# Spreading the dense work of a decoder evenly beside its expert gathers, and tying VectorE's part of each dense step behind the dot of the gather ahead of it

## The chip, the cores and the metric

The kernel runs on one core of one Trainium2 chip. The metric is the device time of one execution in microseconds (us). A run of this kernel can tell a change of about 0.2% from none.

## The reference

Two layers, 512 tokens of width 1024, float32. Each layer is a token mixer and a retrieval of experts, both closed by a LayerNorm:

```
m  = x @ w_in                                   # 7168 columns: q, k, v, two LRU branches, two gates
ya = DiffAttention(q, k, v)                     # 8 heads, two softmax maps each
yr = RG-LRU(conv4(x-branch)) * gelu(gate branch)
x  = LayerNorm(alpha*x + (sigmoid(ga)*(ya@w_br_attn) + sigmoid(gr)*(yr@w_br_lru)) @ w_out)
# PEER: 8 heads; top 16 of 128 first keys, top 16 of 128 second keys, top 16 of their sums
e, g = chosen experts (16 per head, 128 per token), softmax of their scores
x  = LayerNorm(alpha*x + sum_e g[e] * gelu(x . peer_u[e]) * peer_v[e])
```

Each token thus reads 128 rows of `peer_u` and `peer_v`. The two tables lie side by side in one table `uv` of 2048 columns.

## The kernel before

Tokens stand in four blocks of 128. One gather is one indirect DMA (L819): for one of the 128 expert places it brings a row of `uv` to each of the 128 tokens of a block, 128 x 2048 floats. There are 2 layers x 4 blocks x 128 = 1024 gathers, in eight buffers (`gather`, tag `uv`). VectorE forms the dot with x (L822); for each pair of gathers ScalarE takes the gelu (L829), VectorE multiplies by g (L784), and the second half of the row is added up with that weight, either on VectorE (`acc`, L790) or on ScalarE and TensorE together (a diagonal matrix `dg`, L794, and two matmuls into `pv`, L796). `Load` keeps rough sums of TensorE's, VectorE's and the DMA's work and decides which of the two (L788). A pair is finished after the first dot of the next pair has been written.

The dense work is everything else: the mixer of a pair of blocks (projections L253 and L275, attention L349 on, LRU L459 on, gated merge L524 on), and the route (L673): queries (L656), key scores (L663), the sixteen best of each (`top16`, L710 on) and the choice of the sixteen best sums (`choose`, L723 on: candidate sums L736, three operations of 128 x 864 per head at L753, L756 and L758, and the cast L761 that writes the indices `e` which the gathers read). The route scores both blocks of a pair and chooses for the first of them; `route_late` chooses for the second.

Three generators are interleaved in `run` (L841 on): the gathers, `dense()`, and `late()`. Each dense step yields when it would like to come, in gathers. `PLAN` gives the bounds for each pair of blocks: mixer from j0 to j1, route to j2, late choice to j3. Within such a stretch a step's place goes by fixed costs that the steps yield (L853). What this writes is only the source order. A list scheduler then orders each engine's queue by that priority and by its own estimate of when operands are ready, so an instruction can be placed well ahead of where the generator wrote it. Engines run their queues in order. Weights come by SP's DMA queue (L230), five buffers deep.

The first pair of blocks of layer 0 runs before any gather can start, since its route gives the first indices; the last 240 or so gathers have no mixer beside them.

Of the kernel before, what the change touches and what calls it, by code (L numbers as in the profile page):

```python
# [13 lines left out]
F32R = mybir.dt.float32r  # L14
# [4 lines left out]
ALU = mybir.AluOpType  # L19
# [3 lines left out]
D = 1024  # L23
# [24 lines left out]

PLAN = (
    (0, [0, 1], 0, 0, 30, 110),
    (0, [2, 3], 30, 222, 270, 370),
    (1, [0, 1], 270, 470, 526, 620),
    (1, [2, 3], 526, 730, 786, 880),
)
MAXN = P * max(len(p[1]) for p in PLAN)
C_CHUNK = 1.75
HGS = {True: (1, 2, 2, 2), False: (2, 2, 2, 2)}


def weave(a, b, pace=1.0):
# [12 lines left out]
class Load:  # L75
# [6 lines left out]
    def __init__(self, nc):  # L82
        self.nc = nc
        self.seen = 0
        self.begin()

    def begin(self):
        self.pe = self.dve = self.dma = 0.0

    def update(self):  # L90
        todo = self.nc.cur_bb.bb.instructions
        for inst in todo[self.seen :]:
            name = type(inst).__name__
            if not inst.outs or not hasattr(inst.outs[0], "ap"):
                continue
            size = lambda o: math.prod(n for _, n in list(o.ap)[1:])
            n = size(inst.outs[0])
            if inst.engine == mybir.EngineType.PE:
                self.pe += 0.013 + n / 2400 if inst.ins[0].dtype == F32R else 0.009 + n / 596
            elif inst.engine == mybir.EngineType.DVE:  # L100
                n = max([n] + [size(o) for o in inst.ins if hasattr(o, "ap")])
                self.dve += 0.15 + n / 960 + 0.08 * (len(inst.outs) > 1 or "Match" in name)
            elif name == "InstDMACopy":
                self.dma += n * min(P, list(inst.outs[0].ap)[0][1]) * 4 / 420e3
                self.dma = max(self.dma, max(self.pe, self.dve) - self.AHEAD)
                self.pe = max(self.pe, self.dma - self.SLACK)
                self.dve = max(self.dve, self.dma - self.SLACK)
        self.seen = len(todo)


class Acts:
# [9 lines left out]
class Decoder:  # L121
# [551 lines left out]
    def route(self, l, blocks, h0):  # L673


        if h0 == 0:
            self.begin_top()
        for HG in HGS[h0 > 0]:
            sv, si = self.top_tiles(HG)
# [17 lines left out]
    def route_late(self, l, blocks):  # L697
        sv, si = self.top
        h0 = 0
        for HG in HGS[False]:  # L700
            r = slice(2 * h0, 2 * (h0 + HG))
# [3 lines left out]
    def top_tiles(self, HG):  # L705
        sv = self.t2.tile([P, 2 * max(HGS[False]), TOPK], F32, name="sv", tag="sv")
        si = self.t2.tile([P, 2 * max(HGS[False]), TOPK], U32, name="si", tag="si")
        return sv[:, : 2 * HG], si[:, : 2 * HG]
# [65 lines left out]
    def experts(self, l, b, G=2):  # L774
        nc, pp = self.nc, self.pp
        x = self.xn[b]
        pv = None
        e, g = self.e[b], self.g[b]
        began = [False]

        def finish(j0, q, uvs):

            w = pp.tile([P, G], F32, name="w", tag="w")
            nc.vector.tensor_tensor(w, q, g[:, j0 : j0 + G], ALU.mult)  # L784
            for i in range(G):
                j, t = j0 + i, uvs[i]
                self.load.update()
                vector = self.load.dve + 1.22 <= self.load.pe + 1.72  # L788
                if j == P - 1 or (vector and j < P - 2):
                    nc.vector.scalar_tensor_tensor(out=acc, in0=t[:, D:], scalar=w[:, i : i + 1],  # L790
                                                   in1=acc, op0=ALU.mult, op1=ALU.add)
                else:
                    dg = pp.tile([P, P], F32, name="dg", tag="dg")
                    nc.scalar.activation(dg, self.ident, AF.Copy, scale=w[:, i : i + 1])  # L794
                    for half in range(2):
                        nc.tensor.matmul(pv[:, half], dg,  # L796
                                         t[:, D + half * 512 : D + (half + 1) * 512],
                                         start=not began[0], stop=j == P - 2)
                    began[0] = True
            yield  # L800

        prev = iter(())
        for j0 in range(0, P, G):
            if j0 % TOPK == 0:
                yield ("route", l, b, j0 // TOPK)
                if j0 == 0:
                    if (l, b) == (0, 0):
                        self.load.update()
                        self.load.begin()
                    acc = pp.tile([P, D], F32, name="acc", tag="acc", bufs=1)  # L810
                    nc.scalar.activation(acc, x, AF.Copy, scale=ALPHA)
                    pv = self.ps_v.tile([P, 2, 512], F32, name="pv", tag="pv")
            dots = pp.tile([P, G], F32, name="dots", tag="dots")
            q = pp.tile([P, G], F32, name="q", tag="q")
            uvs = []
            for i in range(G):
                j = j0 + i
                t = self.gp.tile([P, 2 * D], F32, name="uvt", tag="uv")
                nc.gpsimd.indirect_dma_start(  # L819
                    out=t, out_offset=None, in_=self.uv,  # L820
                    in_offset=bass.IndirectOffsetOnAxis(ap=e[:, j : j + 1], axis=0))
                nc.vector.scalar_tensor_tensor(out=t[:, :D], in0=t[:, :D], scalar=1.0, in1=x,  # L822
                                               op0=ALU.mult, op1=ALU.mult,
                                               accum_out=dots[:, i : i + 1])
                uvs.append(t)
                if i == 0:
                    next(prev, None)
                else:
                    nc.scalar.activation(q, dots, AF.Gelu_apprx_tanh)  # L829
                yield 1  # L830
            prev = finish(j0, q, uvs)
        for _ in prev:
            pass
        sums = pp.tile([P, 1], F32, name="sums2", tag="sums2")
        nc.vector.scalar_tensor_tensor(out=x, in0=acc, scalar=1.0,
                                       in1=pv.rearrange("p a c -> p (a c)"), op0=ALU.mult,
                                       op1=ALU.add, accum_out=sums)
        self.layer_norm(l, 1, [(b, sums)], LN_EPS, acc)
        self.done.add(("experts", l, b))

    def run(self):  # L841
        nc = self.nc
        self.setup()
        self.cst = [None] * DEPTH
        self.done = set()
        self.load = Load(nc)

        def gathers():
            for l in range(DEPTH):
                for b in range(NB):  # L850
                    yield from self.experts(l, b)

        def paced(steps, total, a, b):  # L853
            cost = 0.0
            for c in steps:
                cost += c
                yield a + (b - a) * min(1.0, cost / total)

        choice = 4 * 6 + 4 * 3


        def dense():
            for k, (l, blocks, j0, j1, j2, _) in enumerate(PLAN):
                if l:
                    yield ("experts", l - 1, blocks[-1])
                nb = len(blocks)
                yield from paced(self.mixer(l, blocks, l == 0 and blocks[0] == 0),
                                 80 * nb * C_CHUNK + 64 * nb + 12, j0, j1)
                if k:
                    yield ("chosen", k - 1)  # L870
                yield from paced(self.route(l, blocks, int(k == 0)), 16 * nb * C_CHUNK + 24 + choice, j1, j2)
                self.done.add(("scored", k))

        def late():
            for k, (l, blocks, _, _, j2, j3) in enumerate(PLAN):
                yield ("scored", k)
                yield from paced(self.route_late(l, blocks), choice, j2, j3)
                self.done.add(("chosen", k))

        streams = [gathers(), dense(), late()]  # L880
        at = [0, 0.0, 0.0]
        wants = [None] * 3
        live = [True] * 3
        while any(live):
            free = [i for i in range(3) if live[i] and (wants[i] is None or wants[i] in self.done)]
            i = min(free, key=lambda i: (at[i], -i))
            wants[i] = None
            c = next(streams[i], None)
            if c is None:
                live[i] = False  # L890
            elif isinstance(c, tuple):
                wants[i] = c
            elif i:
                at[i] = c
            else:
                at[0] += c
# [34 lines left out]
```

## Time and profile before

| | |
|---|---|
| median of 3 runs | 3445.73 us (3443.23 to 3445.84) |
| the profiled execution, its own time | 3443.5 us |
| its span, first to last instruction | 3441.3 us |
| mean granted TensorE clock | 0.933 |
| busy: TensorE, VectorE, ScalarE, GpSimd | 86%, 77%, 36%, 38% |
| read from HBM | 1285.92 MB |

The page cuts the span into 40 slices of 86 us and gives each engine's busy share in tenths, the share of the sixteen DMA engines, and the GB/s they moved. A matmul's end is modelled, so a busy TensorE isn't one at its peak. "Idle before" and "wait" name who released the waiting instruction by the recorded semaphores. Times of stretches are counted from the span's start.

### The profile page before, as it was taken

The page shows a single profiled execution, that of the slowest core. Times are in us where ns is not written, and L with a number is a line of the kernel's source. Part 1 is how long each engine was busy: PE and PEld are TensorE (multiplying, and loading weights), DVE is VectorE, ACT ScalarE, POOL GpSimd, SP SyncE. Part 2 cuts the span into 40 slices and gives each one's busy share as a digit, 9 for nine tenths or more (in the row PEclk, how much of TensorE's full clock was granted, in tenths as well). Part 3 has the DMA queues.
Part 4 walks back from the last instruction along what each step waited for, and adds up shares of the span by engine and source line. Part 5 has one row for each costly group of instructions (what it writes and reads, how often), then busy time and mean ns, then how long its engine had stood idle before and what let it go on. Part 6 is the DMA issues. An engine that isn't in the chain of part 4 may idle for free.

```text
span 3441.3 us, 38208 instructions
## 1 busy us (share of the span) xinstructions
PE 2962.3 (86%) x11832; PEld 1899.5 (55%) x11832; DVE 2660.9 (77%) x6622; ACT 1242.6 (36%) x2851; POOL 1307.3 (38%) x1033
## 2 busy tenths in 40 slices
PE   8997999999997899999996799999998687656655
PEld 8896666777763466677763366666755232212111
DVE  7765989887689577867699569777679965777776
ACT  7852356652122364633122236644122221111111
POOL 0001334444333434434333433433433344565553
PEclk9998999999999999999997999999999799877677
DMA  5455899999999999999998999999999899999997
GB/s 202 155 174 204 332 408 397 414 418 418 418 398 354 380 392 401 393 417 412 418 389 342 412 393 391 401 413 419 418 412 353 312 405 421 421 422 410 421 422 317
DMA packets 219114, 1290.54 MB, mean 375 GB/s; under 512 B 24593, under 2 KB 37137, under 8 KB 87841
## 3 DMA queue, kind: packets, MB, share of 16 engines
q0 software_dynamic: 147456, 1073.81, 77.0%
q1 hardware_dynamic: 71456, 214.30, 16.4%
q8 instruction: 96, 1.57, 0.2%
q14 instruction: 106, 0.86, 0.1%
HBM read 1285.92 MB, written 2.10 MB: 374 GB/s over the span
## 4 chain that ended last, share of the span: by engine, by line
PE 44%; DVE 24%; DMA 19%; issue 6%; POOL 3%; ACT 3%; POOLq 0%; SPq 0%; DVEq 0%; ACTq 0%
DMA uvt<-uv_dram,e 19%; PE ps_mm L253 18%; PE pv L796 16%; DVE uvt L822 8%; POOL uvt L819 3%; DVE acc L790 3%; PE ps_mm L275 3%; PE ps_ln L313 1%; PE ps_qk L253 1%; DVE oh L756 1%; DVE ef L758 1%; PE s L386 1%; DVE oh L753 1%; PE ps_mm L656 1%; PE po L417 1%
## 5 line engine op out<-in xcount | busy, mean ns | idle before, releaser
L819 POOL DMA_INDIRECT uvt<-uv_dram,e x1024 | 1304.7, 1274 | 2101.5 <-PE pv L796 655.1
L796 PE MATMUL pv<-uvt,dg 128*128 128x512 f32 x2712 | 1417.4, 662 | 379.3 <-ACT dg L794 377.8
L822 DVE SCALAR_TENSOR_TENSOR uvt<-uvt,xn 128x1024 f32<-128x1024 f32 x1024 | 1243.8, 1220 | 248.3 <-DMA uvt<-uv_dram,e 244.4
L796 PEld LDWEIGHTS pv<-uvt,dg 128*128 128x128 f32 x2712 | 527.8, 206 | 1094.7 <-ACT dg L794 604.4
L253 PE MATMUL ps_mm<-room_xT,w 128*128 128x256 f32 x2304 | 538.6, 380 | 0.7 <-ACT room_xT L285 0.7
L829 ACT ACTIVATE q<-dots 128x2 f32<-128x2 f32 x512 | 104.1, 203 | 1132.3 <-DVE uvt L822 1117.4
L253 PEld LDWEIGHTS ps_mm<-room_xT,w 128*128 128x128 f32 x2304 | 430.4, 190 | 108.8 <-issue 53.9
L790 DVE SCALAR_TENSOR_TENSOR acc<-uvt,w,acc 128x1024 f32<-128x1024 f32 x346 | 443.6, 1282 | 7.9
L794 ACT ACTIVATE dg<-ident,w 128x128 f32<-128x128 f32 x678 | 257.4, 398 | 290.3 <-DVE w L784 171.1
L784 DVE TENSOR_TENSOR w<-q,g 128x2 f32<-128x2 f32 x512 | 80.7, 158 | 208.9 <-ACT q L829 203.9
L656 PE MATMUL ps_mm<-room_xT,w 128*128 128x256 f32 (+1 forms) x1056 | 241.5, 377 | 0.0
L656 PEld LDWEIGHTS ps_mm<-room_xT,w 128*128 128x128 f32 x1056 | 194.7, 194 | 42.7 <-issue 19.9
L829 ACT ACT_TABLE_LOAD x115 | 147.5, 1283 | 19.6 <-DVE uvt L822 17.0
L238 DVE TENSOR_TENSOR wsp<-raw,wsp 128x1024 fp32r<-128x1024 f32 x80 | 97.1, 1222 | 27.0 <-ACT wsp L237 24.8
L275 PEld LDWEIGHTS ps_mm<-w,room_xT 128*128 128x128 f32 x768 | 90.8, 192 | 8.5 <-issue 7.1
L275 PEld LDWEIGHTS ps_mm<-w,room_m 128*128 128x128 f32 x768 | 89.2, 192 | 9.2 <-issue 8.4
L275 PE MATMUL ps_mm<-w,room_xT 128*128 128x128 f32 x768 | 92.6, 275 | 0.0
L253 PE MATMUL ps_mm<-room_yr,w 128*128 128x256 f32 x384 | 90.1, 380 | 0.0
L253 PE MATMUL ps_mm<-room_ya,w 128*128 128x256 f32 x384 | 89.5, 379 | 0.0
L275 PE MATMUL ps_mm<-w,room_m 128*128 128x128 f32 x768 | 89.3, 275 | 0.0
L237 ACT CAST wsp<-raw 128x1024 fp32r<-128x1024 f32 x80 | 82.7, 1052 | 14.8 <-PE ps_mm L253 7.8
L822 DVE DVE_READ_ACCUMULATOR uvt<-uvt,xn 128x1 f32 x1024 | 84.1, 82 | 0.0
(196 smaller groups left out, 2980.7 us busy)
## 6 DMA issues: line engine op xcount, KB each, us to landing
w<-wpk_dram SPq DMA_DIRECT2D x304, 512.0 KB
raw<-wpk_dram SPq DMA_DIRECT2D x80, 512.0 KB
uvt<-uv_dram,e POOLq DMA_INDIRECT x1024
gw<-gpk_dram SPq DMA_DIRECT2D x32, 128.0 KB
sk<-spk_dram SPq DMA_DIRECT2D x64, 64.0 KB
xn<-x_dram SPq DMA_DIRECT2D x4, 512.0 KB
out_dram<-xn SPq DMA_DIRECT2D x8, 256.0 KB
lq<-lqk_dram SPq DMA_DIRECT2D x2, 128.0 KB
```

Of the source, the lines that this page charges most:

```text
L237: self.nc.scalar.copy(hi, raw)
L238: self.nc.vector.tensor_tensor(lo, raw, hi.bitcast(F32), ALU.subtract)
L253: self.nc.tensor.matmul(ps[:, :n], w, x, start=i == 0, stop=i == len(steps) - 1)
L275: self.nc.tensor.matmul(out[:, i], x(slice(i * P, (i + 1) * P)), w, start=j == 0, stop=j == len(steps) - 1)
L656: nc.tensor.matmul(pq[:, :n], w[:, kc, :], self.acts_x.plain[:, kc, t0 : t0 + n], start=kc == 0, stop=kc == KC - 1)
L784: nc.vector.tensor_tensor(w, q, g[:, j0 : j0 + G], ALU.mult)
L790: nc.vector.scalar_tensor_tensor(out=acc, in0=t[:, D:], scalar=w[:, i : i + 1], in1=acc, op0=ALU.mult, op1=ALU.add)
L794: nc.scalar.activation(dg, self.ident, AF.Copy, scale=w[:, i : i + 1])
L796: nc.tensor.matmul(pv[:, half], dg, t[:, D + half * 512 : D + (half + 1) * 512], start=not began[0], stop=j == P - 2)
L819: nc.gpsimd.indirect_dma_start(out=t, out_offset=None, in_=self.uv, in_offset=bass.IndirectOffsetOnAxis(ap=e[:, j : j + 1], axis=0))
L822: nc.vector.scalar_tensor_tensor(out=t[:, :D], in0=t[:, :D], scalar=1.0, in1=x, op0=ALU.mult, op1=ALU.mult, accum_out=dots[:, i : i + 1])
L829: nc.scalar.activation(q, dots, AF.Gelu_apprx_tanh)
```

## The change

`PLAN` gets other bounds, and for each of the three stretches of a pair a total of work. `paced` no longer adds up the costs that the steps yield: it asks `Load` how much work (TensorE's share weighted by 0.744, plus VectorE's) the step has just issued, and places the next step by that share of the total. While a dense or late step is traced, `tc.issue_after(self.dot)` adds an ordering edge from the latest dot (L822) to each VectorE instruction of the step: the scheduler may not queue it ahead of that dot. It is an order on VectorE's queue alone, no semaphore. The first pair's route takes its heads in groups of 1, 1, 2, 2, 1 instead of 1, 2, 2, 2.

```diff
 PLAN = (
-    (0, [0, 1], 0, 0, 30, 110),
-    (0, [2, 3], 30, 222, 270, 370),
...
-    (1, [2, 3], 526, 730, 786, 880),
+    (0, [0, 1], 0, 0, 75, 190, (1.0, 128.0, 47.0)),
+    (0, [2, 3], 75, 225, 295, 420, (374.0, 142.0, 47.0)),
...
+    (1, [2, 3], 530, 705, 785, 940, (374.0, 142.0, 47.0)),
 )
-HGS = {True: (1, 2, 2, 2), False: (2, 2, 2, 2)}
+HGS = {True: (1, 1, 2, 2, 1), False: (2, 2, 2, 2)}
...
             if inst.engine == mybir.EngineType.PE:
-                self.pe += 0.013 + n / 2400 if inst.ins[0].dtype == F32R else 0.009 + n / 596
+                us = 0.013 + n / 2400 if inst.ins[0].dtype == F32R else 0.009 + n / 596
+                self.pe += us
+                self.work += us * 0.744
             elif inst.engine == mybir.EngineType.DVE:
                 n = max([n] + [size(o) for o in inst.ins if hasattr(o, "ap")])
-                self.dve += 0.15 + n / 960 + 0.08 * (len(inst.outs) > 1 or "Match" in name)
+                us = 0.15 + n / 960 + 0.08 * (len(inst.outs) > 1 or "Match" in name)
+                self.dve += us
+                self.work += us
...
-                nc.vector.scalar_tensor_tensor(out=t[:, :D], in0=t[:, :D], scalar=1.0, in1=x,
-                                               op0=ALU.mult, op1=ALU.mult,
-                                               accum_out=dots[:, i : i + 1])
+                self.dot = nc.vector.scalar_tensor_tensor(
+                    out=t[:, :D], in0=t[:, :D], scalar=1.0, in1=x, op0=ALU.mult, op1=ALU.mult,
+                    accum_out=dots[:, i : i + 1]).ins
...
         def paced(steps, total, a, b):
-            cost = 0.0
-            for c in steps:
-                cost += c
-                yield a + (b - a) * min(1.0, cost / total)
-
-        choice = 4 * 6 + 4 * 3
+            done, begun = 0.0, self.load.update()
+            while next(steps, None) is not None:
+                done += self.load.update() - begun
+                yield a + (b - a) * min(1.0, done / total)
+                begun = self.load.update()
...
-            c = next(streams[i], None)
+            if i and self.dot is not None:
+
+                with self.tc.issue_after(self.dot):
+                    c = next(streams[i], None)
+            else:
+                c = next(streams[i], None)
```

What this does to the order of instructions shows best on VectorE's queue. First the end of the last choice of all: the cast that writes the indices `e_111` of the fourth block in layer 1. Before, on VectorE, it stands after the 757th dot (L822 is the dot, L758 and L756 parts of the choice, L784 the weight of a pair of gathers):

```order
L756 TENSOR_TENSOR oh<-oh,ca 128x864
L753 TENSOR_TENSOR oh<-iota,pf 128x864
L822 SCALAR_TENSOR_TENSOR uvt,dots<-uvt,xn_103 128x1024
L758 TENSOR_REDUCE ef<-oh 128x16
L784 TENSOR_TENSOR w<-q,g_113 128x2
L756 TENSOR_TENSOR oh<-oh,ca 128x864
L822 SCALAR_TENSOR_TENSOR uvt,dots<-uvt,xn_103 128x1024
L758 TENSOR_REDUCE ef<-oh 128x16
L761 CAST e_111<-ef 128x32
L763 TENSOR_TENSOR ef<-tv 128x32
L822 SCALAR_TENSOR_TENSOR uvt,dots<-uvt,xn_103 128x1024
```

In the changed program (its own line numbers: L831 is the dot, L767 the end of the choice, L770 the cast, L799 the sum on VectorE) the same cast stands on VectorE after the 937th dot:

```order
L793 TENSOR_TENSOR w<-q,g_115 128x2
L799 SCALAR_TENSOR_TENSOR acc<-uvt,w,acc 128x1024
L831 SCALAR_TENSOR_TENSOR uvt,dots<-uvt,xn_4854 128x1024 x2
L793 TENSOR_TENSOR w<-q,g_115 128x2
L799 SCALAR_TENSOR_TENSOR acc<-uvt,w,acc 128x1024
L831 SCALAR_TENSOR_TENSOR uvt,dots<-uvt,xn_4854 128x1024
L770 CAST e_111<-ef 128x32
L772 TENSOR_TENSOR ef<-tv 128x32
L774 TENSOR_REDUCE sm_st<-ef 128x2
L831 SCALAR_TENSOR_TENSOR uvt,dots<-uvt,xn_4854 128x1024
```

All four casts of that block's layer-1 choice move, from the 744th, 749th, 753rd and 757th dot to the 821st, 860th, 898th and 937th.

Second the choice of a group of two heads in the last route, on VectorE near the 741st dot. Before, the piece from the candidates' best (L716, L718, L721) to the indices stands in one lump ahead of a dot:

```order
L718 MAX_INDEX pi<-tv,ca 128x8
L767 TENSOR_TENSOR g_114<-ef,sm_st 128x32
L721 MATCH_REPLACE ca<-tv,ca 128x54 x2
L716 MAX tv<-ca 128x8 x2
L718 MAX_INDEX pi<-tv,ca 128x8 x2
L728 CAST fi<-top_17923 128x64
L747 CAST pf<-pi 128x32
L729 TENSOR_SCALAR fi<-fi 128x2x16
L822 SCALAR_TENSOR_TENSOR uvt,dots<-uvt,xn_103 128x1024
L753 TENSOR_TENSOR oh<-iota,pf 128x864 x2
L784 TENSOR_TENSOR w<-q,g_113 128x2
L822 SCALAR_TENSOR_TENSOR uvt,dots<-uvt,xn_103 128x1024
```

In the changed program, near the 740th dot, the same operations (L725, L727, L730) and the three large ones behind them (L762, L765, L767) stand apart, with a dot between them:

```order
L730 MATCH_REPLACE ca<-tv,ca 128x54 x2
L725 MAX tv<-ca 128x8 x2
L727 MAX_INDEX pi<-tv,ca 128x8 x2
L793 TENSOR_TENSOR w<-q,g_113 128x2
L756 CAST pf<-pi 128x32
L831 SCALAR_TENSOR_TENSOR uvt,dots<-uvt,xn_103 128x1024
L762 TENSOR_TENSOR oh<-iota,pf 128x864
L831 SCALAR_TENSOR_TENSOR uvt,dots<-uvt,xn_103 128x1024
L765 TENSOR_TENSOR oh<-oh,ca 128x864
L793 TENSOR_TENSOR w<-q,g_113 128x2
L831 SCALAR_TENSOR_TENSOR uvt,dots<-uvt,xn_103 128x1024
L767 TENSOR_REDUCE ef<-oh 128x16
```

In these rows each gap between two dots now holds one of the large operations; before, the gap after the lump held two at once.

Third the constants of layer 1 (`spa`, a chain of small operations, L212 to L220). Before, VectorE has them in the first mixer, ahead of any gather (L507 and L402 belong to layer 0):

```order
L215 TENSOR_SCALAR spa_9328<-spa_9328 128x8
L214 TENSOR_TENSOR spa_9328<-spa_9328,spz_9327 128x8
L507 SCALAR_TENSOR_TENSOR thx<-thx,xc 128x256
L215 TENSOR_SCALAR spa_9328<-spa_9328 128x8
L216 SCALAR_TENSOR_TENSOR spa_9328<-spa_9328,spz_9326 128x8
L218 TENSOR_TENSOR spa_9328<-spa_9328,spy_9325 128x8
L220 TENSOR_SCALAR sp_9355<-spa_9328 128x8
L402 RECIPROCAL at_st<-at_st 128x2
```

In the changed program VectorE has them around the 298th dot, between the pair weights (L793) and dots (L831) of layer 0's third block (L224 is the step before the last of the chain, L225 to L229 its end):

```order
L224 TENSOR_SCALAR spa_9579<-spa_9579 128x8
L793 TENSOR_TENSOR w<-q,g_114 128x2
L225 SCALAR_TENSOR_TENSOR spa_9579<-spa_9579,spz_9577 128x8
L227 TENSOR_TENSOR spa_9579<-spa_9579,spy_9576 128x8
L831 SCALAR_TENSOR_TENSOR uvt,dots<-uvt,xn_4854 128x1024
L229 TENSOR_SCALAR sp_9606<-spa_9579 128x8
L831 SCALAR_TENSOR_TENSOR uvt,dots<-uvt,xn_4854 128x1024
L793 TENSOR_TENSOR w<-q,g_114 128x2
```

They have left the first 300 us, and stand among the gathers now. TensorE's queue ahead of the first gather is the same in both programs, and so is the whole of SP's queue but for one pair of output stores.

## Rows read from the trace of the kernel before

**Rows 1.** The page's 40 slices: busy tenths of three engines, DMA share, GB/s.
```profile
PE   8997999999997899999996799999998687656655
DVE  7765989887689577867699569777679965777776
DMA  5455899999999999999998999999999899999997
GB/s 202 155 174 204 332 408 397 414 418 418 418 398 354 380 392 401 393 417 412 418 389 342 412 393 391 401 413 419 418 412 353 312 405 421 421 422 410 421 422 317
```

**Rows 2.** The page's DMA queues: packets, MB, share of the sixteen engines.
```profile
q0 software_dynamic: 147456, 1073.81, 77.0%
q1 hardware_dynamic: 71456, 214.30, 16.4%
```

**Rows 3.** Stretches: from:to, length; busy PE, PEld, DVE, ACT, POOL; clock, DMA share, GB/s.
```profile
0.00:303.00 303.00, 279.28 (x2172) 264.10 (x2172) 202.45 (x484) 199.89 (x378) 4.86 (x12) 0.98 0.46 157
303.00:430.00 127.00, 110.73 (x445) 76.94 (x446) 106.94 (x464) 38.55 (x105) 38.99 (x33) 0.95 0.91 348
500.00:600.00 100.00, 97.66 (x435) 67.10 (x434) 93.18 (x236) 57.73 (x127) 40.60 (x32) 1.00 0.99 400
600.00:950.00 350.00, 339.20 (x1571) 248.29 (x1570) 275.27 (x540) 136.23 (x297) 142.60 (x110) 0.99 1.02 417
1060.00:1140.00 80.00, 60.59 (x143) 28.14 (x142) 74.26 (x290) 22.71 (x57) 33.45 (x27) 0.90 0.88 327
1160.00:1480.00 320.00, 309.99 (x1196) 201.13 (x1195) 230.80 (x578) 176.05 (x382) 121.09 (x100) 0.97 0.99 396
1780.00:1890.00 110.00, 78.53 (x226) 42.59 (x225) 110.00 (x406) 26.14 (x71) 41.50 (x32) 0.83 0.92 353
2000.00:2260.00 260.00, 256.22 (x1078) 171.10 (x1076) 214.10 (x498) 154.50 (x314) 98.62 (x82) 1.00 1.00 398
2600.00:2760.00 160.00, 111.35 (x286) 55.07 (x286) 159.53 (x562) 42.92 (x105) 59.51 (x48) 0.85 0.88 322
2823.00:3424.00 601.00, 369.99 (x583) 122.99 (x581) 433.18 (x706) 84.04 (x269) 326.35 (x234) 0.80 1.00 416
303.00:2823.00 2520.00, 2305.52 (x9071) 1510.10 (x9072) 2019.63 (x5425) 955.59 (x2200) 976.07 (x788) 0.96 0.98 394
3424.00:3441.00 17.00, 7.53 (x8) 2.34 (x8) 5.66 (x10) 3.11 (x5) 0.00 (x0) 0.50 0.08 31
```

**Rows 4.** Costliest VectorE groups of 2600:2760: busy us, mean ns, idle before.
```profile
L822 DVE SCALAR_TENSOR_TENSOR uvt<-uvt,xn 128x1024 f32<-128x1024 f32 x49 | 59.5, 1214 | 0.0
L790 DVE SCALAR_TENSOR_TENSOR acc<-uvt,w,acc 128x1024 f32<-128x1024 f32 x14 | 17.8, 1272 | 0.0
L758 DVE TENSOR_REDUCE ef<-oh 128x16 f32<-128x864 f32 x14 | 14.6, 1047 | 0.0
L756 DVE TENSOR_TENSOR oh<-oh,ca 128x864 f32<-128x864 f32 x14 | 14.5, 1051 | 0.0
L753 DVE TENSOR_TENSOR oh<-iota,pf 128x864 f32<-128x864 f32 x14 | 14.4, 1050 | 0.0
L718 DVE FIND_INDEX8 pi<-tv,ca 128x8 uint32<-128x54 f32 x28 | 5.7, 208 | 0.0
...
L716 DVE MAX8 tv<-ca 128x8 f32<-128x54 f32 x28 | 4.8, 205 | 0.0
```

**Rows 5.** The chain of waits in 303:430: start, us, what.
```profile
319.48 9.49 DMA sk<-spk_dram
...
346.30 7.26 DMA uvt<-uv_dram,e
```

**Rows 6.** Waits of VectorE, whole span: total us, times, longest.
```profile
DVE uvt L822 <- DMA uvt<-uv_dram,e: 244.4, 244, 3.2
```

More of the change, by code (lines that the diff above doesn't have):

```diff
@@ L51 @@
 PLAN = (
-    (0, [0, 1], 0, 0, 30, 110),
-    (0, [2, 3], 30, 222, 270, 370),
-    (1, [0, 1], 270, 470, 526, 620),
-    (1, [2, 3], 526, 730, 786, 880),
[4 rows of a table added]
 )
@@ L84, in __init__ @@
         self.seen = 0
+        self.work = 0.0
         self.begin()
@@ L108, in update @@
         self.seen = len(todo)
+        return self.work
 class Acts:
@@ L845, in run @@
         self.done = set()
+        self.dot = None
         self.load = Load(nc)
@@ L853, in paced @@
         def paced(steps, total, a, b):
-            cost = 0.0
-            for c in steps:
-                cost += c
-                yield a + (b - a) * min(1.0, cost / total)
-        choice = 4 * 6 + 4 * 3
+            done, begun = 0.0, self.load.update()
[3 more added lines that the diff above has]
+                begun = self.load.update()
         def dense():
-            for k, (l, blocks, j0, j1, j2, _) in enumerate(PLAN):
+            for k, (l, blocks, j0, j1, j2, _, work) in enumerate(PLAN):
                 if l:
                     yield ("experts", l - 1, blocks[-1])
-                nb = len(blocks)
-                yield from paced(self.mixer(l, blocks, l == 0 and blocks[0] == 0),
-                                 80 * nb * C_CHUNK + 64 * nb + 12, j0, j1)
+                yield from paced(self.mixer(l, blocks, l == 0 and blocks[0] == 0), work[0], j0, j1)
                 if k:
                     yield ("chosen", k - 1)
-                yield from paced(self.route(l, blocks, int(k == 0)), 16 * nb * C_CHUNK + 24 + choice, j1, j2)
+                yield from paced(self.route(l, blocks, int(k == 0)), work[1], j1, j2)
                 self.done.add(("scored", k))
         def late():
-            for k, (l, blocks, _, _, j2, j3) in enumerate(PLAN):
+            for k, (l, blocks, _, _, j2, j3, work) in enumerate(PLAN):
                 yield ("scored", k)
-                yield from paced(self.route_late(l, blocks), choice, j2, j3)
+                yield from paced(self.route_late(l, blocks), work[2], j2, j3)
                 self.done.add(("chosen", k))
```

1 row of the table PLAN is left out of this document.

## The prediction

> **What bounds the kernel now.** I read the page's slices first, then the DMA queues, then stretches, and last the waits. The slices show the DMA at 8 or 9 from the fifth slice to the last but one, with GB/s between 312 and 422 [rows 1]. The reader is to see that a share of 9 is not yet full: it rounds, and the GB/s tell the rest. The gathers are 1073.81 MB in 1024 transfers, 1.0486 MB each, and the loads on SP's queue 214.30 MB [rows 2]. None of these bytes goes away, so the question is only how steadily they flow.
>
> The stretches split the span in three. Up to 303 us no gather can start: TensorE is busy 279 of 303 us. From 303 to 2823 us (gathers 0 to 784, with dense work beside them) the core moves 394 GB/s. From 2823 to 3424 us gathers run alone at 416, which at the rounded edges is the 421 or 422 of the last slices [rows 1, 3]. In between there is a stretch, 600 to 950 us, with dense work and 417 GB/s, TensorE 97% and VectorE 79% busy. So 417 is what this core reaches with dense work beside the gathers, and the middle is under it: 2520 us x (1 - 394/417) = 139 us is all that an even flow could give back.
>
> Where it is lost: three stretches in which VectorE is busy 74 of 80, 110 of 110 and 160 of 160 us, and the DMA moves 327, 353 and 322 GB/s; two in which TensorE is busy 310 of 320 and 256 of 260 us, at 396 and 398 GB/s; and the first 127 us of the gathers at 348 GB/s [rows 3]. A VectorE that is full lets dots come late, buffers come free late, and transfers start late. In the last of the three, VectorE's 160 us hold 49 dots, but also 14 of each of the three large operations of the choice, 43.5 us together [rows 4].
>
> **The change part by part.** Sums go against the profiled execution's own 3443.5 us, of which the span is 3441.3; the median of the runs is 2.2 us above it.
>
> The *late choices move*. Before, the fourth block's layer-1 choice is over at the 757th dot, though its indices are first needed by gather 896; now it is over at the 937th. It has 8 heads. Per head the choice costs 1.05 us three times and two each of 0.208 and 0.205 us, so 3.15 + 0.83 = 3.98 us, and 8 heads 31.8 us [rows 4]. Without it, the stretch 2600 to 2760 has 128 us of VectorE work for its 49 gathers, 2.6 us each; the DMA needs 49 x 1.0486 MB / 417 GB/s = 123 us. VectorE is then no longer far above the DMA, and the route's own part is spread as well (over 80 gathers instead of 56). So I take the stretch to run at the DMA's pace: 160 x (1 - 322/417) = 36.5 us back. The other two are the same case at the ends of the two routes before: 80 x (1 - 327/417) = 17.3 and 110 x (1 - 353/417) = 16.9 us. Together 70.7. From below this is bounded by the late choice's own 31.8 us out of the last stretch and nothing else, from above by the 70.7; I take the 70.7, since nearly all work of the route is spread, not the late choice alone.
>
> The 31.8 us land in gathers 785 to 940. There VectorE is busy 433 of 601 us [rows 3]; some 390 us of that time take 32 more, so it goes to about 80%. Cost nothing; the cover is a DMA at its ceiling. If the cover were gone it would cost the 31.8.
>
> The *first gathers*. The first route is spread over 75 gathers instead of 30. What is lost is 127 x (1 - 348/417) = 21.0 us. Not all of it is VectorE's: the chain of waits there also holds transfers, a subkey load of 9.49 us queued among the gathers and a gather of 7.26 us [rows 5]. And the choices now come close to need: indices for gather 48 are written at dot 43, for gather 16 at dot 11, with eight buffers ahead. I take half, 10.5 us, with ends of -10 and 21.
>
> The *TensorE stretches* lose 320 x (1 - 396/417) = 16.1 and 260 x (1 - 398/417) = 11.8 us. The attention of layer 1 gets no more gathers by the plan (165 and 175 against 200 and 204 for the mixer), but its steps are now placed by issued work and not by fixed prices, which evens TensorE's load. I take half, 14, with ends of 0 and 27.9. The rest of the 139 us is 139 - 21.0 - 70.7 - 27.9 = 19.4, scattered; again half, 9.7.
>
> What is *given back*: the work of the routes now stands in stretches that were light on VectorE. The nearest row for a VectorE at 93% with TensorE at 98% is 500 to 600 us: 400 GB/s [rows 3]. If 250 us of the spread stretches run like that, they lose 250 x (1 - 400/417) = 10 us. Ends 0 and, over 700 us, 29.
>
> The *tie*. A dense operation on VectorE now stands behind the newest dot, and the dot waits for its gather. Queued behind a waiting dot are then the pair's weight, the sums on VectorE and the dense operations; who waits for those is ScalarE and TensorE (transposes of the softmax, gates of the LRU, merges). VectorE waits for gathers 244 times, 244.4 us in all, 1.0 us each and 3.2 at most [rows 6]. No row shows a dense operation behind such a wait that was not there before, so I bound it: VectorE is busy 2020 of 2520 us in the middle, TensorE 2306, so 500 and 214 us are free [rows 3]. Some 120 dense results go from VectorE to TensorE in the three mixers (48 transposes' inputs, 24 each for gates, LRU outputs and merges). At the mean 1.0 us each that is 120 us, inside TensorE's free 214: nothing. At 3.2 us each it is 384, of which 170 stick out. From the other side it can gain, as dots no longer stand behind lumps. I take zero, by the mean row.
>
> The layer-1 constants (28 small operations) leave the first 303 us, where TensorE with an unchanged queue sets the end, and go among the gathers; both cost nothing beside a DMA-bound stretch. 18 sums move from TensorE to VectorE by the balance of `Load`; at 1.27 us [rows 4] that is 23 us on an engine with 500 free.
>
> Sum: 70.7 + 10.5 + 14 + 9.7 - 10 = 95 us. 3443.5 - 95 = 3348.5, plus the 2.2 to the median: 3351, said as 3350 us.
>
> One rule speaks against this. The measured 417 to 422 GB/s [rows 1, 3] are my ceiling. The Trainium skill, "DMA: Bandwidth & Descriptors", section "Specifications", gives about 358 GB/s per core as the HBM's limit. By that figure the middle would already be over its limit at 394, and the sum would be zero: 3446 us. The rows over 358 for whole stretches contradict it here, where one core runs alone.
>
> **The rivals.**
>
> *Even flow all the way.* All 139 us come back: 3443.5 - 139 + 2 = 3307. For it: 350 us at 417 GB/s with both compute engines under load. Against: the first gathers' own chain.
>
> *TensorE takes over.* With VectorE's lumps gone, TensorE in order behind weights and tied operands sets the pace everywhere as in 1160 to 1480 and 2000 to 2260, some 397 GB/s: 2520 x 394/397 = 2501, so 19 us back, 3427. For it: 97 to 98% busy there. Against: TensorE's total, 2306 of 2520 us, leaves the DMA's 2381 us free.
>
> *The tie holds TensorE up.* Each tied result makes TensorE wait, and its sums `pv` stand behind in its queue, so buffers come free late. The price is 120 waits beyond the free 214 us; at 3.2 us each 170 us, and the lumps' gain is eaten too where it would have come from a free TensorE: 3446 + 170 - 95 = 3521. It decides against the kernel from (214 + 95)/120 = 2.6 us per wait. For it: every softmax crosses VectorE three times. Against: waits of 1.0 us, and other matmuls stand between.
>
> *It does not do what it says*: TensorE's and SP's queues aren't tied, and early dense matmuls would keep the flow as uneven as it is: 3446. Against: the order of VectorE shows the choices at their new places.
>
> *The HBM limit* of the mechanism above, the flow already at what the memory gives: 3446; the rows leave it 1 in 100.
>
> **How the numbers follow.** Forecast (3325 to 3385): 0.60. Even flow (under 3325): 0.14. TensorE takes over (3385 to 3436): 0.12. Nothing changes, by either cause: 0.06. The tie: 0.08. Faster by over 0.2% (about what a measurement of this kernel can tell from none) is the first three, 0.86; within, 0.06; slower, 0.08. The range is 3305, the even flow, to 3410, which takes in a part of TensorE's case; it leaves out the rest of that, no change, and the tie, about 2 in 10.
>
> **What would show it.** In the changed profile no stretch of 80 us or more between 303 us and the end of the dense work has VectorE over 97% with the DMA under 360 GB/s; the dip near 2600 to 2760 is gone; gathers end near 3330; TensorE's granted clock has no 0.83 or 0.85 stretch before the last 240 gathers. Right for the first gathers: the first 127 us move over 370 GB/s. Wrong for the tie: TensorE's idle time grows, with VectorE named as what ended it, and dense work runs past gather 785. The prediction is wrong if the middle moves under 403 GB/s.

## The result, and the profile after

The changed kernel takes 3363.91 us (median of 4 runs, 3361.48 to 3367.48) beside 3445.78 us for the kernel before on the same chip (4 runs, 3443.23 to 3446.22). The ratio is 0.9765, 95% interval 0.9748 to 0.9782. That is 82 us less; 95 were forecast. Its span is 3362.3 us.

The page's slices after the change, as in [rows 1]:

```profile
PE   8997988999989989999989899999999875666655
DVE  6765789998877888888768888888767888888776
DMA  5455999999999999999999999999999999999997
GB/s 197 152 176 195 402 407 419 408 384 418 413 417 404 383 410 409 405 409 410 418 396 404 405 409 410 400 418 406 417 406 407 407 401 422 421 417 402 422 422 324
```

The reader is to see that the holes are gone: from the fifth slice to the last but one the lowest figure is 383 GB/s, where it was 312. VectorE is at 6 to 9 there, mostly at 7 or 8, where it ran from 5 to 9.

Stretches of the same clock times, columns as in [rows 3], with the middle and the end parted at 2700 us, close to where gather 784 now falls (2747 us, before 2823):

```profile
303.00:430.00 127.00, 110.53 (x422) 73.22 (x421) 93.73 (x337) 34.31 (x100) 51.20 (x43) 0.95 0.99 401
600.00:950.00 350.00, 340.09 (x1530) 252.92 (x1530) 310.42 (x661) 166.05 (x357) 144.78 (x112) 0.99 1.00 408
1060.00:1140.00 80.00, 75.35 (x266) 47.22 (x265) 66.25 (x212) 23.71 (x67) 27.96 (x24) 0.98 0.96 386
1160.00:1480.00 320.00, 296.17 (x1113) 187.92 (x1111) 260.87 (x757) 158.12 (x358) 129.07 (x106) 0.97 1.00 408
1780.00:1890.00 110.00, 105.36 (x370) 64.94 (x369) 87.84 (x304) 29.18 (x92) 42.11 (x37) 1.00 1.01 407
2000.00:2260.00 260.00, 247.70 (x1049) 168.25 (x1048) 223.07 (x480) 152.24 (x310) 112.25 (x85) 0.99 1.00 410
2600.00:2760.00 160.00, 133.06 (x351) 65.93 (x352) 139.74 (x462) 44.47 (x121) 74.15 (x61) 0.94 0.99 403
303.00:2700.00 2397.00, 2237.35 (x8990) 1497.13 (x8989) 1965.65 (x5166) 906.21 (x2136) 974.53 (x774) 0.97 1.00 407
2700.00:3345.00 645.00, 403.92 (x603) 134.81 (x602) 522.27 (x1028) 106.49 (x300) 354.48 (x251) 0.76 1.00 414
```

The three stretches in which VectorE was full go from 327, 353 and 322 GB/s to 386, 407 and 403, the first gathers from 348 to 401, the two TensorE stretches from 396 and 398 to 408 and 410. The one stretch that was at 417 falls to 408: its VectorE is busy 310 of 350 us now, 275 before [rows 3]. The middle as a whole goes from 394 to 407. By the dots' times in the two traces, gathers 0 to 784 take 2437 us instead of 2516, gathers 784 to the last dot 599 instead of 600; so the whole gain is in the middle. The same clock times no longer hold quite the same gathers and dense work, so what is read from them is rough by some us.

### The profile page after: what moved, and what is told of

It reads as the page before. It is cut to its first block, busy times and chain, and to the rows that moved or that the text cites. A ratio compares the mean times of both kernels' runs of the same rounds, so it can differ in the third digit from the quotient of the medians.

```text
span 3362.3 us, 38056 instructions
## 1 busy us (share of the span) xinstructions
PE 2927.5 (87%) x11760; PEld 1898.5 (56%) x11760; DVE 2693.0 (80%) x6658; ACT 1216.2 (36%) x2820; POOL 1332.2 (40%) x1033
## 4 chain that ended last, share of the span: by engine, by line
PE 46%; DMA 21%; DVE 15%; issue 8%; ACT 5%; POOL 4%; POOLq 0%; SPq 0%; DVEq 0%; ACTq 0%
DMA uvt<-uv_dram,e 21%; PE pv L805 17%; PE ps_mm L262 14%; DVE uvt L831 6%; PE ps_mm L665 5%; POOL uvt L828 4%; PE ps_mm L284 3%; DVE acc L799 2%; PE ps_ln L322 1%; PE ps_qk L262 1%; PE po L426 1%; PE ps_sc L672 1%; PE s L395 1%; PE pg L498 1%; ACT L838 1%
## 5 line engine op out<-in xcount | busy, mean ns | idle before, releaser
L828 POOL DMA_INDIRECT uvt<-uv_dram,e x1024 | 1329.7, 1299 | 1999.1 <-PE pv L805 716.5
L805 PE MATMUL pv<-uvt,dg 128*128 128x512 f32 x2640 | 1376.3, 661 | 304.0 <-ACT dg L803 303.6
L831 DVE SCALAR_TENSOR_TENSOR uvt<-uvt,xn 128x1024 f32<-128x1024 f32 x1024 | 1244.0, 1219 | 191.9 <-DMA uvt<-uv_dram,e 187.6
L805 PEld LDWEIGHTS pv<-uvt,dg 128*128 128x128 f32 x2640 | 519.9, 207 | 978.3 <-ACT dg L803 491.2
L799 DVE SCALAR_TENSOR_TENSOR acc<-uvt,w,acc 128x1024 f32<-128x1024 f32 x364 | 467.3, 1284 | 10.5
L803 ACT ACTIVATE dg<-ident,w 128x128 f32<-128x128 f32 x660 | 250.3, 398 | 256.5 <-DVE w L793 134.8
L793 DVE TENSOR_TENSOR w<-q,g 128x2 f32<-128x2 f32 x512 | 80.6, 158 | 238.4 <-ACT q L838 236.9
L668 ACT COPY pqT<-ps_mm 128x256 f32<-128x256 f32 (+1 forms) x66 | 24.0, 364 | 180.3 <-PE ps_mm L665 155.0
```

Source lines behind the costliest of these rows:

```text
L805: nc.tensor.matmul(pv[:, half], dg, t[:, D + half * 512 : D + (half + 1) * 512], start=not began[0], stop=j == P - 2)
L828: nc.gpsimd.indirect_dma_start(out=t, out_offset=None, in_=self.uv, in_offset=bass.IndirectOffsetOnAxis(ap=e[:, j : j + 1], axis=0))
L831: self.dot = nc.vector.scalar_tensor_tensor(out=t[:, :D], in0=t[:, :D], scalar=1.0, in1=x, op0=ALU.mult, op1=ALU.mult, accum_out=dots[:, i ...
```

## Experiments

All are compared with the kernel before on their own chip; its medians lay between 3445.41 and 3447.43 us. Theory A: VectorE's lumps held the transfers up, and the tie is what moves them. Theory B: the even portions are what counts, by a steadier TensorE.

### The two parts apart

Spread without the tie:

```diff
-            if i and self.dot is not None:
+            if False:
```

> The changed kernel without the ordering edges: new bounds, portions and head groups, but VectorE's part of a dense step is free to be queued early. In its order the last choice of layer 1 is over at the 756th dot (757th before the change, 937th with it). Theory A (VectorE's lumps set the gain, and only the tie moves them): the stretches with VectorE full and the DMA under 360 GB/s come back around gathers 450 to 490 and 710 to 760; only the first gathers keep their gain, about 3415 us. Theory B (the even portions set the gain, by a steadier TensorE, the tie is incidental): about 3365 us.

Measured: 3454.24 us, ratio 1.0022 (1.0010 to 1.0033): slower than before the change. Three stretches of its profile, columns as in [rows 3]:

```profile
1050.00:1150.00 100.00, 76.98 (x253) 44.80 (x251) 98.39 (x411) 28.46 (x76) 38.49 (x30) 0.93 0.95 359
1800.00:1900.00 100.00, 85.05 (x293) 51.62 (x292) 99.90 (x395) 28.23 (x82) 34.98 (x29) 0.97 0.96 372
2660.00:2760.00 100.00, 66.62 (x143) 30.14 (x142) 96.08 (x345) 27.42 (x62) 37.53 (x30) 0.80 0.84 310
```

VectorE is full again, and the DMA down again. Theory B has fallen. Theory A holds in kind and not in size: 3415 us was expected. The first 127 us of gathers kept their gain (399 GB/s), the first 64 gathers half of it (215 us by the dots' times; 199 in the changed kernel, 231 before), and gathers 64 to 320 took 837 us instead of 822 before. Why the new bounds cost 15 us there without the tie was not tried.

The tie without the spread: the kernel before, with the changed lines of `run` and of the dot alone.

```diff
+                self.dot = nc.vector.scalar_tensor_tensor(...).ins
...
+            if i and self.dot is not None:
+                with self.tc.issue_after(self.dot):
+                    c = next(streams[i], None)
...
```

> The kernel before with the ordering edges alone: old bounds, fixed prices, old head groups. In its order the last choice is over at the 857th dot. Theory A: most of the lumps go, the first gathers don't gain; about 3385 us. Theory B: no change, about 3446 us, or slower if tied results make TensorE wait (rival of the prediction: over 3446 us).

Measured: 3397.25 us, ratio 0.9861 (0.9845 to 0.9878), 48 us less than before; 60 were expected. Most of what it lacks against the changed kernel stands in two stretches:

```profile
303.00:430.00 127.00, 107.83 (x439) 75.95 (x438) 103.83 (x462) 38.01 (x104) 34.75 (x32) 0.95 0.91 335
2660.00:2760.00 100.00, 87.92 (x257) 46.67 (x255) 88.42 (x348) 29.15 (x81) 39.40 (x34) 0.93 0.87 346
```

The first gathers are as slow as before (335 beside 348 GB/s): the old bounds want the first route within 30 gathers, and the new ones gave 399 there without the tie. Near the end of the dense work a dip is left. So the parts don't add: the tie alone gives 48, the spread alone costs 8, together they give 82. Beyond the first gathers the new bounds gained only where the tie makes VectorE keep to them.

### Which steps the tie has to hold

Edges on the late choices alone (`i == 2` in place of `i`), and on mixer and route alone (`i == 1`):

> The changed kernel with the edges on the late choices alone (mixer and route free). In its order the route's first choices are early again (gathers 768 to 864 written at the 708th to 738th dot, with the scoring of both blocks), the late ones stay late (937). Theory A (lumps of VectorE, whoever makes them): part of the gain, since the late choices make up 32 of the some 72 us of choosing of a pair and the scoring adds more; about 3405 us. Theory A2 (the late choices alone are the lump): about 3365 us. Rival (the tie of the mixers costs something, as TensorE waits for tied results): under 3364 us.

> The changed kernel with the edges on mixer and route alone; the late choices are free, and in its order the last is over at the 804th dot, behind the end of the mixers' and routes' work, in the stretch where gathers run alone. Theory A: the late choices of layer 1's fourth block fall into a stretch where VectorE has room, those of the other blocks are nearly where the plan has them (404, 653): 3365 to 3380 us. Theory A2: the lump of the late choices comes back, over 3400 us.

Measured: 3434.43 us (0.9965, 0.9953 to 0.9978) with late choices tied alone; 3376.55 us (0.9791, 0.9773 to 0.9809) with mixer and route tied alone. The first, at the three ends of routes:

```profile
1050.00:1150.00 100.00, 87.26 (x296) 53.09 (x296) 98.67 (x396) 27.79 (x82) 37.38 (x30) 0.95 0.96 375
1800.00:1900.00 100.00, 81.48 (x255) 46.64 (x254) 98.02 (x393) 29.03 (x78) 34.97 (x30) 0.93 0.94 360
2600.00:2700.00 100.00, 81.77 (x265) 47.37 (x264) 96.98 (x380) 27.95 (x79) 33.12 (x30) 0.93 0.90 341
```

The lumps are there although no late choice is in them: scoring and the first block's choices fill VectorE by themselves. So the late choices are the small part (13 us when untied; by the dots' times, 12 of them behind gather 784) and mixer and route the large one (70 us, where theory A expected some 41). These lumps are not all of the 70: by the three stretches (386, 406 and 408 GB/s in the changed kernel) they cost 30. The rest is lost in the mixers between them. First the kernel before, then the late choices tied alone, then the changed kernel:

```profile
430.00:1050.00 620.00, 599.55 (x2646) 425.34 (x2645) 516.28 (x1236) 257.83 (x576) 250.88 (x194) 0.99 1.01 410
1150.00:1800.00 650.00, 622.41 (x2530) 421.67 (x2528) 481.17 (x1206) 265.87 (x607) 247.66 (x201) 0.97 1.00 403
1900.00:2600.00 700.00, 664.43 (x2708) 440.32 (x2706) 529.02 (x1207) 279.01 (x627) 267.01 (x225) 0.98 1.01 408
```

```profile
430.00:1050.00 620.00, 584.01 (x2515) 407.59 (x2514) 513.25 (x1226) 251.70 (x557) 244.21 (x190) 0.97 0.99 399
1150.00:1800.00 650.00, 615.30 (x2467) 410.65 (x2467) 477.71 (x1155) 254.89 (x592) 248.96 (x201) 0.96 0.99 397
1900.00:2600.00 700.00, 660.23 (x2667) 436.89 (x2668) 539.44 (x1220) 269.84 (x612) 282.98 (x225) 0.97 1.00 403
```

```profile
430.00:1050.00 620.00, 578.04 (x2484) 405.65 (x2483) 531.93 (x1251) 249.13 (x558) 252.75 (x198) 0.96 1.00 408
1150.00:1800.00 650.00, 610.72 (x2469) 411.41 (x2468) 515.14 (x1352) 255.24 (x599) 256.79 (x208) 0.97 1.00 409
1900.00:2600.00 700.00, 661.65 (x2709) 443.69 (x2708) 573.04 (x1384) 283.42 (x633) 290.83 (x224) 0.98 1.00 408
```

With mixer and route untied, the mixers lose (620 x 9 + 650 x 12 + 700 x 5)/417 = 40 us against the changed kernel, although VectorE is not full there. From 1150 to 1800 us it is busy for 98% or more in 3 of 65 pieces of 10 us (6 in the changed kernel), TensorE for 99% or more in 47 (35 in the changed kernel). So the tie, which orders VectorE's queue alone, also goes with an evener TensorE. That this is what brings the 40 us back is not shown: no run ties the mixer without the route.

The second kernel, with mixer and route tied alone, has its lump at the end instead; first it, then the changed kernel, in the same stretch:

```profile
2700.00:2800.00 100.00, 66.83 (x124) 25.73 (x122) 97.59 (x347) 29.54 (x62) 41.95 (x34) 0.84 0.91 360
```

```profile
2700.00:2800.00 100.00, 72.65 (x135) 26.93 (x134) 85.02 (x250) 23.08 (x59) 50.01 (x40) 0.85 0.99 405
```

The late choices of the fourth block run in one go there, where gathers are alone and VectorE has room on average, and still cost 100 x (405 - 360)/417 = 11 us. Room on average does not help a lump.

### Portions and head groups

Fixed prices inside the new bounds, the rest as changed:

```diff
-            done, begun = 0.0, self.load.update()
-            while next(steps, None) is not None:
-                done += self.load.update() - begun
-                yield a + (b - a) * min(1.0, done / total)
-                begun = self.load.update()
+            cost = 0.0
+            for c in steps:
+                cost += c
+                yield a + (b - a) * min(1.0, cost / total)
...
```

> The changed kernel with the old fixed prices for the portions inside each stretch; new bounds, tie and head groups stay. In its order the last choice is over at the 902nd dot. Theory A: VectorE's work per gather is nearly as even, so 3360 to 3375 us. Theory B: the portions are what counts, so most of the gain goes, over 3400 us.

Measured: 3387.96 us (0.9833, 0.9813 to 0.9853), 24 us over the changed kernel; at most 11 were expected. It is lost in the second mixer:

```profile
600.00:950.00 350.00, 332.77 (x1527) 251.04 (x1523) 305.80 (x643) 161.14 (x343) 129.21 (x103) 0.99 0.97 391
```

391 GB/s beside the changed kernel's 408, with both engines a little less busy: gathers 128 to 192 take 228 us instead of 205. So the measured portions are worth something of their own once the tie is there, about a quarter of the whole gain.

Old head groups in the first route (`HGS = {True: (1, 2, 2, 2), ...}`):

> The changed kernel with the first pair's route in head groups 1, 2, 2, 2 as before the change. In its order the indices of gather 32 are written after the 32nd dot, so nothing can be in flight then. Theory A with a stall for indices: one emptying of the buffers, about 15 to 25 us slower than the changed kernel, 3380 to 3390 us, all of it before 450 us of the span. Rival (the group sizes are incidental): 3364 us.

Measured: 3369.76 us (0.9782, 0.9759 to 0.9806). The interval overlaps the changed kernel's, so the times don't tell the two apart. In the profile the stall is there, but small; first this kernel, then the changed one:

```profile
370.00:430.00 60.00, 55.83 (x208) 35.92 (x207) 40.99 (x131) 14.03 (x46) 20.48 (x18) 1.00 0.92 373
```

```profile
370.00:430.00 60.00, 58.18 (x214) 37.50 (x215) 45.76 (x173) 15.22 (x51) 23.84 (x19) 1.00 1.02 416
```

60 x (416 - 373)/417 = 6 us, not the expected 15 to 25. The expected emptying did come: GpSimd issues no gather from 395.0 to 409.5 us, and from about 407 to 411 us next to nothing moves. This kernel's GB/s from 400 to 412 us, in 40 slices of 0.3 us:

```profile
GB/s 389 382 410 437 410 437 437 437 437 410 437 355 410 437 369 381 376 200 162 130 72 51 36 17 10 0 27 0 0 0 0 0 0 0 0 0 0 328 109 82
```

It was the price that was too high: some 4 us without transfers and a slow fall ahead of them.

### What is left between 407 and 417 GB/s

Nine gather buffers and three for weights, and its control, eight and three (the cut shows the first; the control has the first pair of lines alone):

```diff
-        self.wp = pool("weights", 5)
+        self.wp = pool("weights", 3)
...
-        self.gp = pool("gather", 8)
+        self.gp = pool("gather", 9)
```

> The changed kernel with nine gather buffers and three weight buffers (nine beside five don't fit). For what is left between 407 and 417 GB/s beside dense work. Theory C (a buffer is held some 8 us after its dot beside dense work and under 5 us without, so too few gathers are in flight): against the kernel of eight gather and three weight buffers it is 20 to 50 us faster. Theory D (the rest is TensorE and VectorE being late on average): no difference between these two.

> The changed kernel with three weight buffers instead of five, the control of the one before. Weights are prefetched two deep less, so 3364 us or some tens slower.

Measured: 3351.64 us (0.9728, 0.9708 to 0.9748) with nine, 3371.27 us (0.9778, 0.9758 to 0.9797) with eight, 20 us apart on one chip. Nine buffers, then eight, in the same three stretches of the mixers:

```profile
430.00:1050.00 620.00, 581.10 (x2498) 403.45 (x2497) 534.49 (x1279) 250.45 (x561) 262.99 (x200) 0.98 1.01 411
1150.00:1800.00 650.00, 610.77 (x2496) 414.33 (x2495) 519.55 (x1375) 256.95 (x605) 267.09 (x210) 0.98 1.01 413
1900.00:2600.00 700.00, 667.21 (x2750) 450.94 (x2749) 577.00 (x1379) 284.18 (x637) 296.64 (x228) 0.98 1.01 413
```

```profile
430.00:1050.00 620.00, 578.20 (x2476) 401.34 (x2475) 530.70 (x1268) 248.55 (x555) 258.68 (x197) 0.97 1.00 407
1150.00:1800.00 650.00, 609.93 (x2462) 411.34 (x2462) 513.84 (x1352) 256.13 (x600) 265.35 (x209) 0.97 1.00 408
1900.00:2600.00 700.00, 660.48 (x2709) 442.80 (x2708) 573.18 (x1379) 283.19 (x632) 288.74 (x224) 0.98 1.00 408
```

So about half of what was left comes back with a ninth buffer. In the changed kernel's trace a buffer's next gather is issued 7.4 us after its dot ended (mean of gathers 64 to 700), and 5.0 us among the last gathers (850 to 1000). That time alone does not set the flow: in the kernel before it is 6.9 us, at 394 GB/s. The kernel with nine is the fastest of the study, 96 us under the kernel before.

The same buffers in the kernel before the change:

> The kernel before with nine gather and three weight buffers. Theory A: a ninth buffer carries one more gather over a lump, but a stretch with VectorE full stays at VectorE's pace, so it gains no more than the changed kernel does from it, 0 to 20 us: 3425 to 3446 us. Rival (the lumps only cost because buffers run out): 3400 us or less.

Measured: 3444.76 us (0.9993, 0.9984 to 1.0003): no change that shows. Two of its stretches:

```profile
1780.00:1890.00 110.00, 78.93 (x236) 43.53 (x234) 110.00 (x426) 28.18 (x75) 42.24 (x32) 0.87 0.93 355
2600.00:2760.00 160.00, 110.14 (x290) 55.24 (x289) 159.83 (x569) 41.15 (x102) 58.57 (x47) 0.85 0.87 324
```

355 and 324 GB/s beside 353 and 322 [rows 3]: where VectorE is full, a ninth buffer changes little. The zero is a sum of two things. The first dot ends at 315.7 us instead of 307.6, as it does at 313.4 instead of 309.6 in the changed kernel with nine and three (313.8 with eight and three, so this is the price of the weight buffers). Behind it, gathers 0 to 784 take 2509 us instead of 2516. So the ninth buffer gives some 7 us of gathers here, and 19 in the changed kernel (2420 us with nine, 2438 with eight).

Longer mixers in layer 1, with eight and five buffers and then with nine and three:

```diff
-    (1, [0, 1], 295, 460, 530, 680, (339.0, 142.0, 47.0)),
-    (1, [2, 3], 530, 705, 785, 940, (374.0, 142.0, 47.0)),
+    (1, [0, 1], 295, 475, 545, 690, (339.0, 142.0, 47.0)),
+    (1, [2, 3], 545, 735, 815, 960, (374.0, 142.0, 47.0)),
```

> The changed kernel with layer 1's bounds later: 295, 475, 545, 690 and 545, 735, 815, 960, so its mixers get 180 and 190 gathers instead of 165 and 175, and the last choice is over at the 957th dot. Theory A carried on (the less dense work per gather, the nearer the DMA is to 417 GB/s): 10 to 20 us under the changed kernel, 3345 to 3355 us. Rival (what is left is no matter of density; the first route's indices and the buffers set it): 3360 to 3370 us.

> The later bounds together with nine gather and three weight buffers. If the two gains add: 3335 to 3345 us; if both take the same slack: about 3350 us, as nine and three alone.

Measured: 3362.91 us (0.9760, 0.9744 to 0.9776) and 3355.66 us (0.9738, 0.9722 to 0.9755): no better than the same buffers without it. The gain of theory A did not come, as the rival had it: more room for layer 1's mixers does not bring the rest back. With eight and five the stretch 1150 to 1800 us moves 412 GB/s (409 in the changed kernel), but 1900 to 2600 us moves 405 (408):

```profile
1900.00:2600.00 700.00, 647.93 (x2596) 427.19 (x2595) 559.71 (x1325) 285.73 (x627) 287.73 (x226) 0.96 1.00 405
```

TensorE has 52 us free there and VectorE 140, and the DMA is no nearer to 417.

Finishing a pair one dot later:

```diff
-                if i == 0:
+                if i:
                     next(prev, None)
-                else:
                     nc.scalar.activation(q, dots, AF.Gelu_apprx_tanh)
```

> The changed kernel with the finish of a pair traced behind the second dot of the next pair instead of the first, so each buffer is kept about one gather's time (some 3 us) longer, and VectorE has one more dot before it needs the gelu. Theory C (too few gathers in flight beside dense work): slower by 15 to 40 us, as one buffer fewer. Rival (VectorE's waits for the gelu, 195 us beside the dense work, are what is left): faster by 10 us or more.

Measured: 3377.43 us (0.9806, 0.9790 to 0.9822), 14 us slower than the changed kernel. It settles neither theory. VectorE's waits for the gelu, which the edit was to shorten, went from 195 to 225 us between 303 and 2700 us, so the rival was not tried. And the next gather is issued 7.7 us after the dot instead of 7.4, not 3 us later, so the 14 us are not shown to come from theory C either.

## Why the prediction was right, and where its sizes were off

- *The bound.* Right: bytes are the same, and the gain is the middle's flow, 394 to 407 GB/s; 409 was forecast (2520 us x 394 / 2425 us). The 416 GB/s of the end before the change is a mean of slices from 405 to 422 [rows 1], not 421 or 422 at rounded edges; the sum does not use it.
- *The lumps of VectorE*, 70.7 us. The mechanism was right for these stretches: taking away the tie brought both lumps and time back. The size was too high. At the same clock times the three stretches still lose 80 x 31/417 + 110 x 10/417 + 160 x 14/417 = 14 us, so 57 came back. Taking the whole route and not the late choices alone was right: with late choices tied alone the lumps stand, and cost 30 us. Calling the late choice's new place free was right as long as it is spread; in one lump it costs 11 us. VectorE is busy 522 of 645 us at the end, 81%; about 80% was said.
- *The first gathers*, 10.5 us. They lose 127 x 16/417 = 5 us instead of 21, so 16 came back: half was too little. A closer margin of the indices (old groups) costs 6 us by its stretch.
- *The TensorE stretches*, 14 us: 320 x 9/417 + 260 x 7/417 = 11 us are still lost of 27.9, so 17 came back. Most of it was given back beside them: over the three whole mixers the flow went from 410, 403 and 408 GB/s to 408, 409 and 408, which is 6 us in all.
- *Given back*, 10 us. The stretch that ran at 417 runs at 408, which alone is 350 x 9/417 = 8 us; the middle runs at about 407 almost everywhere and has no stretch of its own for the loss. The TensorE stretches, the scattered loss and what is given back make 14 + 9.7 - 10 = 14 us in the sum; the mixers measured 6.
- *The sum.* The traces' middle gained 79 us: some 57 in the lumps, 16 in the first gathers, 6 in the mixers, beside 70.7, 10.5 and 14. Two terms were too high and one too low, so the total came nearer than its terms: that part is luck. The two that were too high have one ground: the sum took 417 for what dense work allows in all stretches. About half of the difference comes back with a ninth buffer; for the rest no run gave a cause.
- *The tie costs nothing.* Right. TensorE's free time in the middle fell from 214 us in 2520 to 160 in 2397, and its waits on VectorE grew little. Waits of TensorE in the changed kernel, 303 to 2700 us (total us, times, longest):

```profile
PE pv L805 <- ACT dg L803: 71.1, 52, 5.4
...
PE pg L498 <- DVE xc L492: 11.1, 7, 2.7
...
PE pt L421 <- DVE pr L416: 5.5, 4, 2.9
PE ps_mm L262 <- DVE mth L544: 5.5, 3, 2.5
```

The tie's rival put the turning point at 2.6 us for each of 120 results. All waits of TensorE that end with VectorE, the last three rows among them, are 27 in number and 56 us together in this stretch; in the kernel before, from 303 to 2823 us, they were 12 and 40 us.

- *TensorE takes over*, at 397 GB/s: wrong, the middle moves 407; three of its slices are still under 400 (384, 383 and 396). *No effect*: wrong. *The HBM limit*: wrong; the end still runs at 421 and 422 GB/s in single slices.
- The signs named beforehand hold but for one. In stretches of 80 us taken every 10 us up to gather 784, VectorE is never over 94% busy, the flow never under 379 GB/s and the granted clock never under 0.87; the first 127 us move 401 GB/s, over 370. The exception: the gathers' last dot ends at 3346 us, not near 3330.

## What to carry to other kernels

Where a list scheduler sits between a plan and the queues, a plan of places is a wish: read the built order for where the work ends up before judging the plan, and tie what has to wait. When transfers bound a kernel and buffers are few, an engine with room on average can still cost time wherever its work comes in one long lump. A resource that is worth little before such a change (here a ninth buffer, 7 us of the gathers' time) can be worth more after it (19 us), so try it again.

## What the runs showed that was not expected

Moving the plan without the tie made the kernel slower (1.0022), although VectorE's and TensorE's work was nearly the same (2680 us busy beside 2661, and 2959 beside 2962); in the three mixers it moved 400, 399 and 399 GB/s, where the kernel before moved 410, 403 and 408. And a core alone keeps 407 GB/s for 2.4 ms with TensorE and VectorE at 93% and 82% busy (411 to 413 in the mixers with nine buffers), but did not get back to the 417 that one stretch of the kernel before had at 79% of VectorE; loosening layer 1's mixers by a tenth changed nothing in the time, a ninth buffer did.
